# Reading the moving operand of every 512-column product in turn from the two halves of its columns

## The chip, the cores and the metric

The kernel runs on one core of one Trainium2 chip. The metric is the device time of one execution in microseconds (us), from runs of the whole program. A profiled execution gives a span (first to last instruction), and its own time stands beside that span below. TensorE is called PE, its weight loads PEld, VectorE DVE, ScalarE ACT, GpSimd POOL, and SP is the engine that issues most DMAs.

## The reference

One encoder layer with three parallel branches, on two sequences of 256 tokens each (512 token columns in all), width 1024, in float32:

```python
h = _rmsnorm(x, attn_norm_gain)
proj = h @ w_in                      # -> gdn qkv, decay, gates, mla latents, memory query, merge gates
# branch A: conv + SiLU on q, k, v; bidirectional chunked gated delta rule, 8 heads; gated norm
o_gdn = _rmsnorm(o_fwd + o_bwd, gdn_norm_gain) * silu(z_gdn)
# branch B: latent attention, 8 heads, rotary part; branch C: 4-head attention into 256 memory tokens
merged = (gates[:, :, 0] * (o_gdn @ w_br_gdn)
          + gates[:, :, 1] * (o_mla @ w_br_mla)
          + gates[:, :, 2] * (o_mem @ w_br_mem))
y = _rmsnorm(x + merged @ w_out, final_norm_gain)
```

## The kernel before

**Layout.** Activations are feature-major: a tile holds 128 features as partitions and all 512 tokens as columns. Each operand of a large product is split into a high and a low float32r part, and a product is the sum of three: high x high, low x high and high x low. `gemm` (L234) makes one 128x512 output tile: it loads a piece of weights (`weight`, L199: a DMA to `wr`, ACT rounds it to `wh`, DVE makes the remainder `wl`), then issues 3 x nk matmuls into one PSUM bank, nk being the number of 128-row blocks of the contraction (8, 4, 3 or 2). The weights are the stationary operand (128 columns, loaded anew for every matmul) and the activations `xs[k][j]` the moving operand, 512 columns read one after the other. There are 97 such tiles with nk = 8, 8 with nk = 4, 12 with nk = 3, 8 with nk = 2, and the narrow one of the rotary key: 2,604 matmuls at L246. The other 512-column products have the same form: `mem_v` (L399, 96), `mla_v` (L688, 48), the decay products of `gdn_prep` (L809, 8), `kk` in `gdn_in` (L971, 96) and the output projection (L1256, 168, and 48 more of 256 columns). `mem_v`, `mla_v` and the output projection have the weights as moving operand and the tokens as stationary one.

**Stages.** `front` (0 to 369 us in the profile) computes the memory keys and values, the norm, the latents and both attentions, with product tiles from a list `self.fill` put between the attention's steps. `middle` (369 to 761 us) runs the delta rule. `back` (from 761 us) multiplies the eight `xg` tiles (the normed delta-rule output of each head) by the branch weights (`bg`), merges and runs the output projection `y`. The tiles `bm` (branch B's projection) are the last of the fill list; `gemm` puts the matmuls of `bg` that need `xg7` last within each tile: 21 of 24 come before them.

**Order of PE in the middle.** It is written out by hand in `weave` (L1513). Chains of dependent steps are generators: `lane` 0 and 1 (the solves of the even and the odd heads), `heads_load`, `heads_in`, `heads_out`, `heads_norm`. A step yields two numbers, the PE time that it takes and the time until its next step is due, both in us of a clock that the planner keeps (`self.now`). While the next due step lies in the future, matmuls of the fill list are issued, each of which moves that clock on by the number that `gemm` yields:

```python
            if at[c] > self.now:
                cost = next(fill, None)
                self.idle += at[c] - self.now if cost is None else 0
                self.now = at[c] if cost is None else self.now + cost
```

When nothing of the list may be issued, the planner's clock jumps to the next due step. PE itself executes the order that results and waits only for true results. The due times on which the steps named later rest: head h is loaded once head h-3 has been read out (`while h > self.out + 2`), and counts as loaded 11 us later; `gdn_in` then has due times of 2.5, 2, 8, 6, 6 and 3 us; `gdn_solve` 7 and 7.5, then 6.5 us after each of seven steps (`u`, `xs`, `us`, `x`, `u`, `xs`, `us`); `gdn_out` (`o`, L1121) follows, 13 us after head 7's `o` comes its sum of squares `so` (L1137), and `gdn_norm` 10 and 6 us later. The fill list has conditions too (`can`, L1502): the `bm` tiles wait for all parts of `xa`; the last part is loaded once head 7's first `u` is due (`7 in self.started`) and may be split `XAT` = 14 us after that.

Of the kernel before, what the change touches and what calls it, by code (L numbers as in the profile page):

```python
# [31 lines left out]
        w.reshape(k // P, P, c // P, P).transpose(2, 1, 0, 3)).reshape(c // P, P, k)  # L32

def _pieces(w):

    k, c = w.shape
    return np.ascontiguousarray(
        w.reshape(k // 256, 2, P, c // 512, 512).transpose(3, 0, 2, 1, 4)).reshape(
            c // 512, k // 256, P, 1024)  # L40

def _consts():
# [42 lines left out]
def prep(i):  # L86

    f = {k: np.asarray(v) for k, v in i.items()}
    x = np.concatenate([f["x_prompt"][0], f["x_sample"][0]], 0)
    mem = np.concatenate([f["mem_prompt"][0], f["mem_sample"][0]], 0)  # L90
    w = f["w_in"][0]

    def fm(a):
        return np.ascontiguousarray(a.T.reshape(KD, P, T).transpose(1, 0, 2))

    def tm(a):
        return np.ascontiguousarray(a.reshape(4, P, D).transpose(1, 0, 2))

    def col(a):
        return np.ascontiguousarray(a.reshape(-1, P).T)  # L100

    qu = f["w_q_up"][0].reshape(384, 8, 192)
    rope = [qu[:, 4 * g:4 * g + 4, 128 + 32 * h:160 + 32 * h].reshape(384, P)
            for g in range(2) for h in range(2)]
    ku = f["w_kv_up"][0].reshape(256, 8, 256)
    mkv = f["w_mem_kv"][0]
    w8 = np.concatenate([
        _chunks(mkv[:, :512]),
        _chunks(w[:, O_QKV:O_QKV + 3072]),
        _chunks(w[:, O_ZG:O_ZG + 1024]),  # L110
        _chunks(w[:, O_CQ:O_CQ + 384]),
        _chunks(w[:, O_CKV:O_CKV + 256]),
        _chunks(w[:, O_ZM:O_ZM + 1024]),
        _chunks(w[:, O_QM:O_QM + 512]),
        _chunks(w[:, O_ZE:O_ZE + 512]),
        _chunks(w[:, O_G:O_G + 3072]),
        _chunks(f["w_br_gdn"][0]), _chunks(f["w_br_mla"][0])], 0)
    kr = np.concatenate([w[:, O_CKV + 256:O_CKV + 320], w[:, O_AB:O_AB + 32]], 1)
    kr = np.ascontiguousarray(kr.reshape(KD, P, 96).transpose(1, 0, 2)).reshape(P, KD * 96)
    prm = np.concatenate([  # L120
        col(f["attn_norm_gain"][0]), col(f["mem_norm_gain"][0]),
        f["conv_w"][0].reshape(5, 24, P).transpose(2, 1, 0).reshape(P, 120),
        np.broadcast_to(f["a_log"][0].reshape(1, 16), (P, 16)),
        np.broadcast_to(f["dt_bias"][0].reshape(1, 16), (P, 16)),
        col(f["gdn_norm_gain"][0]), col(f["q_norm_gain"][0]), col(f["kv_norm_gain"][0])], 1)
    a = {
        "xT": fm(x), "xn": tm(x), "memT": fm(mem),
        "cst": _CST, "sum": _SUM, "prm": np.ascontiguousarray(prm), "rope": _rope_tables(),
        "w8": w8, "w4": _chunks(f["w_br_mem"][0]),
        "w3": np.concatenate([  # L130
            _chunks(np.ascontiguousarray(qu[:, :, :128]).reshape(384, 1024))]
            + [_chunks(r) for r in rope], 0),
        "w2": _chunks(np.ascontiguousarray(ku[:, :, :128]).reshape(256, 1024)),
        "wkr": kr,
        "wvm": _pieces(mkv[:, 512:])[0],
        "wv": _pieces(np.ascontiguousarray(ku[:, :, 128:]).reshape(256, 1024))[:, 0],
        "wo": _pieces(f["w_out"][0]),
        "fg": f["final_norm_gain"].reshape(1, D),
    }
    return {k: np.ascontiguousarray(v) for k, v in a.items()}  # L140
# [16 lines left out]
class Layer:  # L157
# [76 lines left out]
    def gemm(self, src, nk, xs, name, m=P, ps=None):  # L234

        nc = self.nc
        hi, lo = self.weight(src, nk * m, name)
        ps = self.ps_gm("gm_" + name) if ps is None else ps
        n = 0
        order = [(p, k) for p in ((hi, 0), (hi, 1), (lo, 0)) for k in range(nk)]  # L240
        last = {"bm": 5, "bg": 7, "qm": 4}.get(name[:2])
        if last:

            order.sort(key=lambda o: o[1] >= last)
        for (a, j), k in order:
            nc.tensor.matmul(ps[:m], a[:, k * m:(k + 1) * m], xs[k][j],  # L246
                             start=n == 0, stop=n == 3 * nk - 1)
            n += 1
            yield 0.234
        return ps  # L250

    def add_square(self, acc, src, k, eng=0):
# [103 lines left out]
    def mem_v(self):  # L356
# [28 lines left out]
        for k, (raw, wr) in enumerate(raws):  # L385
            hl = self.pk.tile([P, 2, 512], F32R, tag="kq", bufs=8, name=f"mh{k}")
            hi = self.p0.tile([P, 1024], F32R, tag="wh", bufs=2, name=f"wh_vm{k}")
            lo = self.p0.tile([P, 1024], F32R, tag="wl", bufs=2, name=f"wl_vm{k}")
            if k:
                nc.scalar.activation(hi[:, :512], wr, AF.Copy)  # L390
            else:
                nc.vector.tensor_scalar(hi[:, :512], wr, 1.0, None, ALU.mult)
            rnd = self.split(raw, hl[:, 0], hl[:, 1], self.mg[:, k:k + 1])
            nc.vector.tensor_tensor(lo[:, :512], wr, hi[:, :512].bitcast(F32), op=ALU.subtract)
            ms.append((hl[:, 0], hl[:, 1]))
            for i, (a, b) in enumerate(((0, hi), (1, hi), (0, lo))):
                for tb in range(4):
                    t = slice(tb * P, (tb + 1) * P)
                    nc.tensor.matmul(vps[tb], ms[k][a][:, t], b[:, :512],  # L399
                                     start=k == 0 and i == 0, stop=k == 7 and i == 2)  # L400
            with self.tc.issue_after(rnd.ins) if k == 0 else nullcontext():
                self.add_square(acc, raw, k, 1)
# [21 lines left out]
    def mem_kt(self, h):  # L424
            nc, A, ms, rb = self.nc, self.A, self.mem_xs, self.rb
            ps = self.gemm_fm(A["w8"][C_KM + h], 8, ms, f"km{h}")
            kt = self.tb(f"kmt{h}")
            nc.scalar.activation(kt, ps, AF.Copy)
            nc.vector.tensor_tensor(kt, kt, rb, op=ALU.mult)
            t = self.big(h, f"km{h}")  # L430
            hi, lo = t[:, 0], t[:, 1]
# [57 lines left out]
    def rotate(self, dst, src, table):  # L489

        n = table.shape[0]
        self.nc.vector.tensor_tensor(dst.rearrange("p (s t) -> p s t", s=2), src.rearrange("p (s t) -> p s t", s=2),
                                     table.unsqueeze(1).to_broadcast([n, 2, 256]), op=ALU.mult)

    def rope_key(self):

# [9 lines left out]
        nc.scalar.activation(abT[64:96], ps[64:96], AF.Copy)  # L506
        t = self.tb("krt")
        u = self.tb("kru")
        self.rotate(t[0:64], ps[0:64], cs[0:64])
        self.rotate(u[0:32], ps[32:64], sn[32:64])  # L510
        self.rotate(u[32:64], ps[0:32], sn[0:32])
        nc.vector.tensor_tensor(t[0:32], t[0:32], u[0:32], op=ALU.subtract)
        nc.vector.tensor_tensor(t[32:64], t[32:64], u[32:64], op=ALU.add)
        self.ks1 = self.pa.tile([P, 512], F32R, name="ks1")
# [135 lines left out]
    def mla_rope(self, g):  # L650
# [5 lines left out]
        qs2 = self.pa.tile([P, 2, 512], F32R, tag="qs2", bufs=1, name=f"qs2{g}")  # L656
        for j, (p1, p2, op) in enumerate(((pa, pb, ALU.subtract), (pb, pa, ALU.add))):
            t, u = self.tb("rt"), self.tb("ru")
            self.rotate(t, p1, self.cos)
            self.rotate(u, p2, self.sin)  # L660
            nc.vector.tensor_tensor(t, t, u, op=op)
            hi = self.pa.tile([P, 512], F32R, tag="Qn", bufs=4, name=f"rh{g}{j}")
            lo = self.pa.tile([P, 512], F32R, tag="Qn", bufs=4, name=f"rl{g}{j}")
# [11 lines left out]
    def mla_v(self, g):  # L675
# [4 lines left out]
        for tb in range(4):  # L680
# [4 lines left out]
            n = 0  # L685
            for a, j in ((hi, 0), (hi, 1), (lo, 0)):
                for k in range(2):
                    nc.tensor.matmul(ps, self.kl[k][j][:, t], a[:, k * 512:(k + 1) * 512],  # L688
                                     start=n == 0, stop=n == 5)
                    n += 1  # L690
            vh = self.pa.tile([P, 512], F32R, tag="V", bufs=8, name=f"vh{g}{tb}")
# [4 lines left out]
    def mla_qk(self, hh, between):  # L696
        A = self.A
        r = []
        for w, nk, xs, n in ((A["w2"], 2, self.kl, "kn"), (A["w3"], 3, self.ql, "qn")):
# [6 lines left out]
            else:  # L706
                hi = self.pa.tile([P, 512], F32R, tag="Qn", bufs=4, name=f"{n}h{hh}")
                lo = self.pa.tile([P, 512], F32R, tag="Qn", bufs=4, name=f"{n}l{hh}")
            self.split(ps, hi, lo)
            r += [hi, lo]  # L710
        return r

# [64 lines left out]
    def gdn_prep(self, g):  # L777
# [12 lines left out]
        for d in range(2):  # L790
# [15 lines left out]
            yield 0.0, 4.0  # L806
            dp = self.ps_ms(d, f"dp{g}{d}")
            for i in range(2):
                nc.tensor.matmul(dp, self.bd, rhs[i], start=i == 0, stop=i == 1)  # L809
            nc.vector.tensor_tensor(ed, ed, dp, op=ALU.add)  # L810
            nc.scalar.activation(ed, ed, AF.Exp)
            eds.append(ed.rearrange("p (w i) -> p w i", i=32))
            yield 0.47, 0.0
# [125 lines left out]
    def gdn_in(self, hh):  # L939
# [24 lines left out]
        for s in range(2):  # L964
            pc = []
            hi, lo = hl[s]
            for cch in range(2):
                k = slice(cch * P, (cch + 1) * P)
                ps = self.ps_kk(f"kk{hh}{s}{cch}")
                for i, (a, b) in enumerate(((hi, hi), (hi, lo), (lo, hi))):  # L970
                    nc.tensor.matmul(ps, a[:, k], b, start=i == 0, stop=i == 2)  # L971
                pc.append(ps.rearrange("p (a t) -> p a t", a=2))
                yield 0.70, 6.0 * cch
            for a in range(2):
                for d in range(2):
                    for cp in range(2):
# [224 lines left out]
    def branch_mem(self, d):  # L1201
# [1 line left out]
        nc = self.nc  # L1203
        gt = yield from self.gate(2, d)
        ps = yield from self.gemm(self.A["w4"][d], 4, self.xe, f"be{d}")
        nc.vector.scalar_tensor_tensor(gt, gt, 1.0, ps, ALU.add, ALU.mult)
        nc.sync.dma_start(self.d_m[d], gt)

    def gate_in(self, j, d):
# [12 lines left out]
    def gated(self, d, gt, ps):  # L1222

        nc = self.nc
        nc.vector.scalar_tensor_tensor(gt, gt, 1.0, ps, ALU.add, ALU.mult)  # L1225
        nc.gpsimd.tensor_tensor(self.merged[d], self.merged[d], gt, op=ALU.add)  # L1226

    def branch(self, j, d, xs, w, name):
# [4 lines left out]
    def output(self):  # L1233
# [17 lines left out]
        def product(ps, hi, lo, j, tb, c0=0, c1=512):  # L1251
            t = slice(tb * P, (tb + 1) * P)
            n = 0
            for q in range(2):
                for a, b in ((0, hi), (1, hi), (0, lo)):
                    nc.tensor.matmul(ps, xs[2 * j + q][a][:, t], b[:, q * 512 + c0:q * 512 + c1],  # L1256
                                     start=j == 0 and n == 0, stop=j == 3 and n == 5)
                    n += 1

# [355 lines left out]
```

## Time and profile before

| what | value |
|---|---|
| median of 3 runs | 859.25 us (858.84 to 859.51) |
| profiled execution | 859.05 us, its span 857.3 us |
| PE busy | 845.6 us (99%), 4,822 matmul records |
| PEld / DVE / ACT / POOL busy | 698.4 / 573.4 / 451.9 / 145.4 us |
| mean DMA rate | 135 GB/s |
| granted TensorE clock | 0.999 |

A matmul's recorded duration is longer than the distance to the next one, since matmuls overlap in the pipeline; the price of one is read from the starts of successive rows. One product of plain float32 operands shows as two matmul records. In rows of the timeline neighbouring instructions of one kind are merged: `x8` are eight of them, and the first number is the first one's start. A name such as `gm_qkv` is the output of the tile `qkv`.

### The profile page before, as it was taken

The numbers are of one execution on the slowest core, as the hardware profiler recorded it, in microseconds if no ns is written. First come the engines' busy times: TensorE is split into PE (matmuls) and PEld (weight loads), VectorE is DVE, ScalarE is ACT, GpSimd is POOL, SyncE is SP. The second block draws the span as 40 slices with busy tenths as digits, with TensorE's granted clock in tenths as the row PEclk, the third lists the DMA queues.
The fourth block names the chain that finished last, engine by engine and source line by source line (L and its number), as shares of the span: only waits on it lengthen the run. The fifth ranks groups of instructions, "written<-read, shape, count | busy, mean of one in ns | idle before, by whom it ended". The sixth has DMA issues, their size and how long they took to land.

```text
span 857.3 us, 13230 instructions
## 1 busy us (share of the span) xinstructions
PE 845.6 (99%) x4822; PEld 698.4 (81%) x4822; DVE 573.4 (67%) x1021; ACT 451.9 (53%) x891; POOL 145.4 (17%) x135
## 2 busy tenths in 40 slices
PE   9999999999999999999999999999999999999997
PEld 7878888888888888878788888888888888888886
DVE  7776347687599998457689998684555544346543
ACT  7655455455474465546775748666663632223232
POOL 0200111000100002072101254213110002332121
PEclk9999999999999999999999999999999999999999
DMA  9422222442425525363334365546445447375332
GB/s 326 141 79 87 86 81 68 139 138 75 103 77 164 137 90 146 116 191 129 109 103 122 117 189 174 152 134 180 132 122 160 138 134 250 118 241 160 116 98 99
DMA packets 68273, 116.10 MB, mean 135 GB/s; under 512 B 24048, under 2 KB 31600, under 8 KB 68208
## 3 DMA queue, kind: packets, MB, share of 16 engines
q1 hardware_dynamic: 46560, 104.51, 38.6%
q10 hardware_dynamic: 21648, 10.75, 4.6%
q8 instruction: 38, 0.62, 0.3%
q14 instruction: 27, 0.22, 0.1%
HBM read 95.09 MB, written 16.99 MB: 131 GB/s over the span
## 4 chain that ended last, share of the span: by engine, by line
PE 95%; DVE 2%; ACT 1%; issue 1%; DMA 1%; POOL 0%; POOLq 0%; ACTq 0%; DVEq 0%; SPq 0%
PE gm_qkv L246 16%; PE gm_g L246 16%; PE gm_z L246 8%; PE gm_bm L246 5%; PE gm_bg L246 5%; PE gm_za L246 5%; PE y L1256 5%; PE vm L399 3%; PE gm_be L246 3%; PE gm_qm L246 3%; PE gm_km L246 3%; PE kk L971 3%; PE o L1121 2%; PE gm_qn L246 2%; PE gm_cq L246 2%; PE s_a L308 2%
## 5 line engine op out<-in xcount | busy, mean ns | idle before, releaser
L745 DVE SCALAR_TENSOR_TENSOR kq<-cz,prm,kq 128x510 f32<-128x510 f32 (+1 forms) x64 | 48.1, 752 | 6.0 <-ACT kq L738 5.0
L246 PE MATMUL gm_qkv<-hh,wh_qkv 128*128 128x512 f32 x192 | 51.1, 400 | 0.5 <-ACT wh_qkv L210 0.5
L246 PE MATMUL gm_g<-hl,wh_g 128*128 128x512 f32 x192 | 51.5, 399 | 0.0
L246 PE MATMUL gm_g<-hh,wl_g 128*128 128x512 f32 x192 | 51.3, 398 | 0.0
L246 PE MATMUL gm_g<-hh,wh_g 128*128 128x512 f32 x192 | 51.1, 401 | 0.1
L246 PE MATMUL gm_qkv<-hh,wl_qkv 128*128 128x512 f32 x192 | 50.3, 397 | 0.0
L246 PE MATMUL gm_qkv<-hl,wh_qkv 128*128 128x512 f32 x192 | 49.7, 396 | 0.0
L214 DVE TENSOR_TENSOR wl_qkv<-wr_qkv,wh_qkv 128x1024 fp32r<-128x1024 f32 x24 | 31.1, 1297 | 25.9 <-ACT wh_qkv L210 10.1
L214 DVE TENSOR_TENSOR wl_g<-wr_g,wh_g 128x1024 fp32r<-128x1024 f32 x24 | 30.1, 1254 | 22.0 <-PE gm_g L246 11.7
L246 PEld LDWEIGHTS gm_qkv<-hl,wh_qkv 128*128 128x128 f32 x192 | 35.8, 188 | 8.2
L246 PEld LDWEIGHTS gm_qkv<-hh,wh_qkv 128*128 128x128 f32 x192 | 35.3, 188 | 8.9 <-ACT wh_qkv L210 1.2
L246 PEld LDWEIGHTS gm_qkv<-hh,wl_qkv 128*128 128x128 f32 x192 | 35.5, 188 | 7.8
L246 PEld LDWEIGHTS gm_g<-hl,wh_g 128*128 128x128 f32 x192 | 35.4, 188 | 7.7
L246 PEld LDWEIGHTS gm_g<-hh,wl_g 128*128 128x128 f32 x192 | 35.3, 188 | 7.5
L246 PEld LDWEIGHTS gm_g<-hh,wh_g 128*128 128x128 f32 x192 | 35.1, 188 | 7.8 <-ACT wh_g L210 0.3
L210 ACT ACTIVATE wh_qkv<-wr_qkv 128x1024 fp32r<-128x1024 f32 x24 | 25.4, 1058 | 29.1 <-PE gm_qkv L246 8.6
L1256 PE MATMUL y<-wh_wo,mh 128*128 128x512 f32 (+1 forms) x144 | 39.9, 370 | 0.0
L210 ACT ACTIVATE wh_g<-wr_g 128x1024 fp32r<-128x1024 f32 x24 | 25.4, 1060 | 26.0 <-PE gm_g L246 11.6
L961 POOL TENSOR_TENSOR kl<-kq,kh 128x512 fp32r<-128x512 f32 x16 | 22.8, 1427 | 94.8 <-ACT kh L959 94.8
L1226 POOL TENSOR_TENSOR mg<-mg,lg 128x512 f32<-128x512 f32 x16 | 27.2, 1700 | 59.0 <-DVE lg L1225 59.0
L246 PE MATMUL gm_bm<-xa,wh_bm 128*128 128x512 f32 x128 | 33.5, 398 | 0.0
L246 PE MATMUL gm_bg<-xg,wh_bg 128*128 128x512 f32 x128 | 32.5, 395 | 0.0
(432 smaller groups left out, 2199.5 us busy)
## 6 DMA issues: line engine op xcount, KB each, us to landing
wr_g<-in_w_dram SPq DMA_DIRECT2D x24, 512.0 KB
wr_qkv<-in_w_dram SPq DMA_DIRECT2D x24, 512.0 KB
e<-d_r SPq DMA_DIRECT2D x64, 96.0 KB
wr_z<-in_w_dram SPq DMA_DIRECT2D x12, 512.0 KB
d_g<-gt_g ACTq DMA_DIRECT2D x16, 256.0 KB
wr_za<-in_w_dram SPq DMA_DIRECT2D x8, 512.0 KB
wr_bm<-in_w_dram SPq DMA_DIRECT2D x8, 512.0 KB
lg<-d_g SPq DMA_DIRECT2D x16, 256.0 KB
```

Source lines behind the costliest of these rows:

```text
L210: self.wround = nc.scalar.activation(hi[:, :n], raw[:, :n], AF.Copy).ins
L214: d = eng.tensor_tensor(lo[:, :n], raw[:, :n], hi[:, :n].bitcast(F32), op=ALU.subtract)
L246: nc.tensor.matmul(ps[:m], a[:, k * m:(k + 1) * m], xs[k][j], start=n == 0, stop=n == 3 * nk - 1)
L308: nc.tensor.matmul(sp[:, qb * 256:(qb + 1) * 256], a, b, start=j == 0, stop=j == n - 1)
L399: nc.tensor.matmul(vps[tb], ms[k][a][:, t], b[:, :512], start=k == 0 and i == 0, stop=k == 7 and i == 2)
L745: nc.vector.scalar_tensor_tensor(ys, zs, self.cw[:, f, m:m + 1], ys, ALU.mult, ALU.add)
L961: nc.gpsimd.tensor_tensor(lo, src, hi.bitcast(F32), op=ALU.subtract)
L971: nc.tensor.matmul(ps, a[:, k], b, start=i == 0, stop=i == 2)
L1121: nc.tensor.matmul(out, ub[:, d, s, cp], rhs, start=n == 0, stop=n == 3)
L1226: nc.gpsimd.tensor_tensor(self.merged[d], self.merged[d], gt, op=ALU.add)
L1256: nc.tensor.matmul(ps, xs[2 * j + q][a][:, t], b[:, q * 512 + c0:q * 512 + c1], start=j == 0 and n == 0, stop=j == 3 and n == 5)
```

## The change

The moving operand of each 512-column product is given as a three-dimensional pattern: column 0 of the first half, column 0 of the second half, column 1 of the first, and so on (`turns`). The output is written to PSUM in the order in which columns arrive, one column after the other (`pairs` gives the output the same shape). So output column 2s + c holds moving column 256c + s. Where the columns were put apart beforehand (even columns in the first half, odd ones in the second), the output has its natural order: the host does that for `xT` and for the weight pieces that are moving operands. Elsewhere the readers of the PSUM tile take it with a step of two elements (`unpaired`) and write natural order (`halves`). Numbers of instructions, DMAs, tiles and buffers are the same. The planner's cost of one matmul goes from 0.234 to 0.217 and that of three `kk` products from 0.70 to 0.65. The attention's 256-column products and the plain-float32 products of the delta rule are not touched.

```diff
+def _halves(a):
+    return np.concatenate([a[..., 0::2], a[..., 1::2]], -1)
 def _pieces(w):
-        w.reshape(k // 256, 2, P, c // 512, 512).transpose(3, 0, 2, 1, 4)).reshape(
+        _halves(w.reshape(k // 256, 2, P, c // 512, 512)).transpose(3, 0, 2, 1, 4)).reshape(
+def turns(x):
+    return x.rearrange("p (c s) -> p s c", c=2)
+def pairs(x):
+    return x.rearrange("p (s c) -> p s c", c=2)
+def halves(x):
+    return x.rearrange("p (c s) -> p c s", c=2)
+def unpaired(x):
+    return x.rearrange("p (s c) -> p c s", c=2)
...
-        "xT": fm(x), "xn": tm(x), "memT": fm(mem),
+        "xT": _halves(fm(x)), "xn": tm(x), "memT": fm(mem),
...
-            nc.tensor.matmul(ps[:m], a[:, k * m:(k + 1) * m], xs[k][j],
+            nc.tensor.matmul(pairs(ps[:m]), a[:, k * m:(k + 1) * m], turns(xs[k][j]),
-            yield 0.234
+            yield 0.217
...
-                    nc.tensor.matmul(vps[tb], ms[k][a][:, t], b[:, :512],
+                    nc.tensor.matmul(pairs(vps[tb]), ms[k][a][:, t], turns(b[:, :512]),
...
-            nc.scalar.activation(kt, ps, AF.Copy)
+            nc.scalar.activation(halves(kt), unpaired(ps), AF.Copy)
...
-            self.rotate(t, p1, self.cos)
-            self.rotate(u, p2, self.sin)
+            self.rotate(t, unpaired(p1), self.cos)
+            self.rotate(u, unpaired(p2), self.sin)
...
-                    nc.tensor.matmul(ps, self.kl[k][j][:, t], a[:, k * 512:(k + 1) * 512],
+                    nc.tensor.matmul(pairs(ps), self.kl[k][j][:, t], turns(a[:, k * 512:(k + 1) * 512]),
...
-            self.split(ps, hi, lo)
+            self.split(unpaired(ps), halves(hi), halves(lo))
...
-                nc.tensor.matmul(dp, self.bd, rhs[i], start=i == 0, stop=i == 1)
-            nc.vector.tensor_tensor(ed, ed, dp, op=ALU.add)
+                nc.tensor.matmul(pairs(dp), self.bd, turns(rhs[i]), start=i == 0, stop=i == 1)
+            nc.vector.tensor_tensor(halves(ed), halves(ed), unpaired(dp), op=ALU.add)
...
-                    nc.tensor.matmul(ps, a[:, k], b, start=i == 0, stop=i == 2)
-                pc.append(ps.rearrange("p (a t) -> p a t", a=2))
-                yield 0.70, 6.0 * cch
+                    nc.tensor.matmul(pairs(ps), a[:, k], turns(b), start=i == 0, stop=i == 2)
+                pc.append(unpaired(ps))
+                yield 0.65, 6.0 * cch
...
-        nc.vector.scalar_tensor_tensor(gt, gt, 1.0, ps, ALU.add, ALU.mult)
+        nc.vector.scalar_tensor_tensor(halves(gt), halves(gt), 1.0, unpaired(ps), ALU.add, ALU.mult)
...
-                    nc.tensor.matmul(ps, xs[2 * j + q][a][:, t], b[:, q * 512 + c0:q * 512 + c1],
+                    nc.tensor.matmul(pairs(ps), xs[2 * j + q][a][:, t],
+                                     turns(b[:, q * 512:(q + 1) * 512])[:, c0 // 2:c1 // 2],
```

More of the change, by code (lines that the diff above doesn't have):

```diff
@@ L491, in rotate @@
         n = table.shape[0]
-        self.nc.vector.tensor_tensor(dst.rearrange("p (s t) -> p s t", s=2), src.rearrange("p (s t) -> p s t", s=2),
-                                     table.unsqueeze(1).to_broadcast([n, 2, 256]), op=ALU.mult)
+        self.nc.vector.tensor_tensor(halves(dst), src, table.unsqueeze(1).to_broadcast([n, 2, 256]), op=ALU.mult)
     def rope_key(self):
@@ L508, in rope_key @@
         u = self.tb("kru")
-        self.rotate(t[0:64], ps[0:64], cs[0:64])
-        self.rotate(u[0:32], ps[32:64], sn[32:64])
-        self.rotate(u[32:64], ps[0:32], sn[0:32])
+        self.rotate(t[0:64], halves(ps[0:64]), cs[0:64])
+        self.rotate(u[0:32], halves(ps[32:64]), sn[32:64])
+        self.rotate(u[32:64], halves(ps[0:32]), sn[0:32])
         nc.vector.tensor_tensor(t[0:32], t[0:32], u[0:32], op=ALU.subtract)
@@ L1224, in gated @@
         nc = self.nc
-        nc.vector.scalar_tensor_tensor(gt, gt, 1.0, ps, ALU.add, ALU.mult)
+        nc.vector.scalar_tensor_tensor(halves(gt), halves(gt), 1.0, unpaired(ps), ALU.add, ALU.mult)
         nc.gpsimd.tensor_tensor(self.merged[d], self.merged[d], gt, op=ALU.add)
```

## The prediction

> **What bounds the kernel now.** I read the page first, then the timeline of PE for the price of one product, then the chain of work for the order of the middle, then stages by window.
>
> ```profile
> span 857.3 us, 13230 instructions
> PE 845.6 (99%) x4822; PEld 698.4 (81%) x4822; DVE 573.4 (67%) x1021; ACT 451.9 (53%) x891; POOL 145.4 (17%) x135
> PE 95%; DVE 2%; ACT 1%; issue 1%; DMA 1%; POOL 0%; POOLq 0%; ACTq 0%; DVEq 0%; SPq 0%
> ```
>
> PE is busy 99% of the span and holds 95% of the chain that ended last. So the price of a product is the price of the kernel, unless something else takes over. That price, from the timeline:
>
> ```profile
> 300.76 0.40 PE L308 MATMUL s_a<-ks,qs 128*128 128x256 f32 x2
> 301.00 0.40 PE L308 MATMUL s_a<-kn,qnh 128*128 128x256 f32 x2
> ...
> 302.78 2.03 PE L246 MATMUL gm_za<-hh,wh_za 128*128 128x512 f32 x8
> 304.65 2.03 PE L246 MATMUL gm_za<-hl,wh_za 128*128 128x512 f32 x8
> 306.51 2.03 PE L246 MATMUL gm_za<-hh,wl_za 128*128 128x512 f32 x8
> 308.38 0.86 PE L246 MATMUL gm_qn<-qlh,wh_qn 128*128 128x512 f32 x3
> ```
>
> From 302.78 to 308.38 are 24 products: 233.3 ns each. A 256-column one takes 0.24 / 2 = 120 ns. So the price is (233.3 - 120) / 256 = 0.443 ns per column and some 7 ns fixed.
>
> Is that the most that PE can do? The plain-float32 products of the read-out tell:
>
> ```profile
> L1121 PE MATMUL o<-e,ub 128*128 128x256 f32 x64 | 19.3, 383 | 0.0
> L1121 PE MATMUL o<-e,ub 128*128 128x128 f32 x64 | 12.3, 274 | 0.0
> 475.16 2.83 PE o L1121 x16
> 507.18 2.62 PE o L1121 x16
> ...
> 588.03 2.81 PE o L1121 x16
> 620.03 2.62 PE o L1121 x16
> ...
> 701.08 2.62 PE o L1121 x16
> 732.93 2.62 PE o L1121 x16
> ```
>
> The 8 heads issue 32 products of 256 and 32 of 128 columns and the trace has 64 of each: two records per product. One head's 16 records bring 8 x 256 + 8 x 128 = 3,072 columns in 2.62 us, 0.853 ns a column. I read a record as two passes over its columns, since the ratio to 0.443 is near two: 0.426 ns a column, 218 ns for 512 with fixed costs included. So PE streams faster when each operand element is used in more than one pass, and the float32r products lose some 16 ns per 512 columns on what feeds them. The loss is there where DVE and ACT are half idle as well:
>
> ```profile
> 820.92 0.39 PE L1256 MATMUL y<-wl_wo,mh 128*128 128x512 f32 x1
> ...
> 822.55 2.49 PE L1256 MATMUL y<-wh_wo,mh 128*128 128x512 f32 x10
> ...
> 806.00:846.00 40.00, 40.00 (x177) 32.50 (x177) 17.72 (x24) 13.46 (x23) 7.94 (x7) 1.00 0.29 97
> ```
>
> 820.92 to 822.55 are 7 products, 233 ns each, with DVE at 17.72 and ACT at 13.46 of 40 us (fourth and fifth numbers) and the full clock (1.00). So it is no contention with other engines; it belongs to the reading of the moving operand, which is what the change touches.
>
> **The change, part by part.**
>
> *The rate.* No row has a moving operand read in turn, so I bound it. Lower end: 217 ns, the rate of the read-out. Upper end: the slowest 512-column stream here,
>
> ```profile
> 1.49 4.28 PE L367 MATMUL zp<-zero 128*128 128x512 f32 x10 [1.49 <-DVE zero L364]
> ```
>
> about 428 ns, at start-up. I take 217: the loss is proportional to columns and goes with the order of feeding, and the read-out shows the array itself able to do it. Saving 16.3 ns on each of 3,020 products (counts in the source: 2,604 + 96 + 48 + 8 + 96 + 168), 49.2 us, and by the 120-ns row about 8 ns on 48 of 256 columns, 0.4 us. [...]
>
> But the saving does not arrive everywhere; by stage:
>
> ```profile
> 0.00:369.40 369.40, 280.82 (x1117) 205.01 (x1118) 1.00 0.39 121
> 369.40:686.00 316.60, 255.00 (x1022) 187.66 (x1022) 1.00 0.47 144
> 369.40:710.40 341.00, 275.34 (x1104) 202.70 (x1104) 1.00 0.46 142
> ```
>
> (windows of L246 alone; the count is behind PE's busy time).
>
> *Front.* 1,117 + 96 + 48 + 4 = 1,265 products x 16.3 = 20.6 us. DVE is nearly full in places:
>
> ```profile
> 240.00:280.00 40.00, 38.80 (x206) 32.65 (x205) 38.79 (x81) 23.63 (x49) 0.00 (x0) 1.00 0.43 126
> 280.00:320.00 40.00, 40.00 (x195) 33.07 (x194) 36.35 (x78) 22.23 (x43) 0.91 (x1) 1.00 0.39 109
> 440.00:480.00 40.00, 40.00 (x288) 32.91 (x287) 37.44 (x80) 25.95 (x62) 5.22 (x4) 1.00 0.40 124
> 480.00:520.00 40.00, 40.00 (x231) 33.45 (x230) 37.77 (x78) 22.86 (x48) 19.18 (x19) 1.00 0.50 151
> ```
>
> From 240 to 320 us DVE needs 75.1 us; at the new rate PE would pass that stretch in about 75. I take off 3 us for waits on DVE, here and where attention steps have less cover. Front: 17.6 us.
>
> *Middle.* Here the planner's due times rule, and they stay. The `o` rows of heads three apart: 475.16 to 588.03, 507.18 to 620.03, 588.03 to 701.08, 620.03 to 732.93, always 112.9 us: load, 11, gdn_in's and gdn_solve's due times, read-out, load again. A faster fill product does not shorten that: more of them go into the same gaps, and the list runs dry sooner. So from the middle's start to head 7's `o` nothing is gained. Before the first `bm` 1,104 products go; at 0.217 they and the shorter `kk` steps fill the gaps that 1,021 fill now, up to about 686. Then:
>
> ```profile
> 681.66 0.61 PE L1078 MATMUL u<-vs,y 128*128 128x128 f32 x4
> 748.47 0.95 PE L1137 MATMUL so<-cst,sq 128*128 128x1 f32 x8
> 759.97 0.69 DVE L226 SCALAR_TENSOR_TENSOR xg<-og,xg 128x512 fp32r<-128x512 f32 x1 [0.70 <-ACT xg L222]
> 761.03 3.43 PE L246 MATMUL gm_bg<-xg,wh_bg 128*128 128x512 f32 x14
> 765.93 0.63 PE L246 MATMUL gm_bg<-xg,wh_bg 128*128 128x512 f32 x2
> ```
>
> `bm` waits for head 7's first `u` (681.7) and 14 us: 695.7 by the plan. In that hole PE has only solve steps; it waits for their true results, which come sooner than the due 6.5 us. I count 6 of the 9.7 us: `bm` from 692. Its 192 products take 41.7 us, the steps among them about 10 (two `o` of 2.62, the rest from 0.4 to 0.9): 743.7. That uses up the cover behind head 7: `so`, planned 13 us behind `o`, now comes after all `bm`. From its end (749.4) to `xg7` (760.7) now pass 11.3 us under cover; then 755. `bg`'s first 21 products last 4.6 us, so PE waits about 6.7 us and the first product on `xg7` starts at 755 instead of 766: 11 us; 7.3 if the whole hole counts. I take 9, less 1.5 for DVE, whose 75.2 us between 440 and 520 meet denser fill: 7.5 us.
>
> *Back.* 171 products of `bg` and 168 of `y`, 339 x 16.3 = 5.5, and 0.4: 5.9 us.
>
> *Readers of PSUM with a step of two.* 24 tiles' ACT and DVE reads, 24 gate products, `dp`, and 128 `kk` reads; not shown, bounded by
>
> ```profile
> L982 DVE SCALAR_TENSOR_TENSOR na<-e,cc,kk 128x256 f32<-128x256 f32 x32 | 15.2, 475 | 8.2 <-PE kk L971 8.1
> L858 DVE TENSOR_TENSOR nd<-nd,kd 128x512 f32<-128x512 f32 x2 | 1.4, 680 | 0.0
> L856 DVE TENSOR_TENSOR dd<-nd,kd 128x512 f32<-128x512 f32 x2 | 2.2, 1099 | 0.0
> ```
>
> From 0 (the same elements, as L858) to 0.42 us per 512 (L856, which writes with a step of 32): DVE work of up to 40 us, spread; where DVE is full, up to 5 us of the time. A gain has no reason. Eight bytes are nearer to none than to 128: I take 0. *Host layout* is outside the measured time; DMAs, queues and weight loads stay (188-ns loads overlap).
>
> *Sum.* 17.6 + 7.5 + 5.9 = 31.0 us: span 826.3; the profiled execution has 1.75 us around its span (859.05), and the median is 0.2 above it: 828 us.
>
> **The rivals.**
>
> *All of it arrives* (49.6 us, 809.5): the true steps of the middle would have to run well ahead of the plan, or the tail after `o` be covered. For it: PE waits only for results. Against: the plan's order puts fill between steps.
>
> *Half the loss goes* (225 ns): front 8.8, back 3; in the middle PE sets the pace until `so`: 1,396 x 8.3 = 11.6 less, then the uncovered 12.2 and not 5: 5 gained. 842. For it: nothing shows that all of the loss is one cause.
>
> *The turn changes nothing at 233 ns.* Then the plan is wrong for it: `so` still comes after all `bm`, at 761, and `xg7` at 773; the first product on it starts 7.2 us late: 866.
>
> *Slower products.* If the loss is paid for each fetch of neighbouring columns, the turn needs more fetches: twice as many cost another 16.3 ns, 249.6 ns and +49 +7: 915. It decides from 7.2 / 3,020 = 2.4 ns below today's price, 231 ns. For it: the extra is per column already; against: no row. [...]
>
> **How the numbers follow.** Forecast 60% (span of its own, 820 to 837: hole and waits at either bound); all arrives 10%; half 13%; no change in rate 6%; slower products 11%. Forecast, all and half are 83%: 809 to 845. A change within 0.2% (1.7 us, what a measurement here tells from none) needs a mixture, 2% from the edge of the last two; slower 15%, faster 83%.
>
> **What would show it.** Eight products in 1.74 us instead of 1.87 (rate); `o` rows still 112.9 us apart (middle); a PE gap of some 5 us before `bg`'s products on `xg7`, ended by DVE at L226, and gaps around 690; L982 still near 475 ns (readers). Wrong if a 512-column product stays above 225 ns, or if `o` rows come closer together.

## The result, and the profile after

The changed kernel takes 829.25 us (median of four runs, 826.32 to 831.36) against 859.38 us (858.84 to 860.04) for the kernel before. The ratio is 0.9647, with a 95% interval from 0.9616 to 0.9677: faster by 30.1 us. The profiled execution took 829.28 us, its span 827.5. The forecast was 828. The total is right to 1.3 us; the way to it inside the middle stage was not.

Line numbers of the changed kernel are higher by 24 or 25: L246 is now L271, L982 is L1006, L1121 is L1145, L1256 is L1280; L1121 in rows of the changed kernel is the solve step `us`. First the page of the changed kernel: span, busy times, and shares of the chain that ended last.

```profile
span 827.5 us, 13240 instructions
PE 799.8 (97%) x4822; PEld 701.0 (85%) x4822; DVE 569.5 (69%) x1021; ACT 448.1 (54%) x891; POOL 141.3 (17%) x135
PE 76%; DVE 8%; ACT 5%; DMA 5%; issue 3%; POOL 1%; SPq 1%; ACTq 0%; POOLq 0%; DVEq 0%
```

PE is busy for 45.8 us less, but the span fell by 29.8 only. PE's share of the chain went from 95% to 76%; DVE's went from 2% to 8%, and ACT's and the DMAs' from 1% to 5% each. So about 46 us were offered, and 16 of them, a third, went into waits that were not there before.

The price of a product, from PE's timeline of the changed kernel (start, length of the group, the instructions):

```profile
305.77 1.89 PE L271 MATMUL gm_za<-hh,wh_za 128*128 128x512 f32 x8
307.50 0.59 PE L271 MATMUL gm_za<-hl,wh_za 128*128 128x512 f32 x2
```

From 305.77 to 307.50 are 8 products in 1.73 us: 216 ns each, where it was 233. That much is as forecast (1.74 for 8). On 3,020 products 17.3 ns are 52 us; of the 6 us that PE's busy time does not show, 1.7 are found below (half the clock), and the rest is not placed. Where the products' saving ended up, by stage, in us (the boundaries are the end of the last `oa`, the first `bg` product and the first `y` product on PE's timeline):

| stage | before | after | gained | forecast |
|---|---|---|---|---|
| front, to the last `oa` | 369.4 | 352.7 | 16.7 | 17.6 |
| middle, to the first `bg` | 391.6 | 380.8 | 10.8 | 7.5 for these two, |
| `bg` | 44.8 | 45.9 | -1.1 | and 2.8 for `bg`'s rate |
| `y` to the end of the span | 51.5 | 48.2 | 3.3 | 3.1 |

Where PE waits, from the list of waits (the waiting instruction, what it waits for, us in total, times, the longest). The kernel before has its two longest in the front and none in the middle:

```profile
PE zp L367 <- DVE zero L364: 1.5, 1, 1.5
PE oa L343 <- DVE za L727: 1.1, 1, 1.1
```

The changed kernel:

```profile
PE us L1121 <- DVE w L1116: 2.5, 2, 1.5
PE kd L847 <- DVE kq L771: 2.5, 1, 2.5
PE gm_bg L271 <- ACT xg L247: 2.3, 1, 2.3
PE kk L995 <- DVE zt_z L1187: 2.3, 1, 2.3
PE gm_g L271 <- ACT wh_g L235: 1.8, 1, 1.8
PE gm_qkv L271 <- ACT wh_qkv L235: 1.6, 2, 1.3
```

The first four are waits of the middle and of `bg`, and three of them are on DVE. A first window of the changed kernel is 400 to 480 us; a second, of the kernel before, lies as far behind its last `oa` (us, then busy time of PE, PEld, DVE, ACT, POOL, then PE's granted clock):

```profile
400.00:480.00 80.00, 77.18 (x663) 67.22 (x663) 76.63 (x161) 50.64 (x113) 13.66 (x11) 1.00 0.36 110
417.00:497.00 80.00, 80.00 (x646) 65.74 (x633) 75.77 (x159) 51.47 (x114) 15.36 (x13) 1.00 0.37 118
```

DVE is busy for 76.6 of these 80 us, but it was so for 75.8 before, and PE never stood idle. So here a full DVE alone did not make PE wait; what counted is when single results came. Shortly before the wait for `kd` (402.7 to 405.2 us), and as the one for `zt_z` (562.5 to 564.8 us) began, DVE itself stood idle, as its rows show:

```profile
398.16 0.75 DVE L769 SCALAR_TENSOR_TENSOR kq<-cz,prm,kq 128x510 f32<-128x510 f32 x1 [4.71 <-ACT kq L762]
...
563.24 0.69 DVE L1177 TENSOR_TENSOR og<-og,rob 128x512 f32<-128x512 f32 x1 [1.73 <-DMA rob<-d_n]
563.97 0.69 DVE L1187 SCALAR_TENSOR_TENSOR zt_z<-zt_z,gm_z 128x512 f32<-128x512 f32 x1
```

In the first case DVE had waited 4.7 us for ACT to start the convolution of `kq`. In the second, `zt_z` stood behind an instruction that waited 1.7 us for a DMA.

The tail of the middle, from PE's timeline of the changed kernel:

```profile
682.21 0.68 PE L1121 MATMUL us<-w,y 128*128 128x128 f32 x4 [1.52 <-DVE w L1116]
...
733.43 3.18 PE L271 MATMUL gm_bg<-xg,wh_bg 128*128 128x512 f32 x14
736.45 1.67 PE L271 MATMUL gm_bg<-xg,wl_bg 128*128 128x512 f32 x7
737.96 3.19 PE L271 MATMUL gm_bg<-xg,wh_bg 128*128 128x512 f32 x14
740.98 1.67 PE L271 MATMUL gm_bg<-xg,wl_bg 128*128 128x512 f32 x7
744.98 1.61 PE L271 MATMUL gm_bg<-xg,wh_bg 128*128 128x512 f32 x3 [2.32 <-ACT xg L247]
746.38 0.63 PE L271 MATMUL gm_bg<-xg,wl_bg 128*128 128x512 f32 x1
```

The hole before `bm` has one wait of 1.5 us in it, not 6. The first 21 products of two `bg` tiles, 42 in all, go before the first product on `xg7`, not 21; so the wait there is 2.3 us, not 6.7. But what follows that wait is slow: 3 products in 1.40 us, from 744.98 to 746.38. The window of the changed kernel behind the wait, with the granted clock third from the end:

```profile
745.05:748.46 3.41, 3.41 (x8) 2.24 (x9) 1.79 (x3) 1.79 (x2) 0.59 (x1) 0.50 0.46 190
```

After the wait PE ran for 3.41 us at half the clock, which costs another 1.7 us.

The readers of PSUM that now step by two take no longer. The group of the 256-column reads of the changed kernel (busy us, mean ns):

```profile
L1006 DVE SCALAR_TENSOR_TENSOR na<-e,cc,kk 128x256 f32<-128x256 f32 x32 | 15.2, 474 | 6.8 <-PE kk L995 6.8
```

It was 475 ns with neighbouring elements. ACT's reads of the same kind (`qnh`, L247) take 586 ns on the mean, 591 before.

### The profile page after: what moved, and what is told of

Its sections match the earlier page's. It is cut to its first block, busy times and chain, and to the rows that moved or that the text cites. A ratio compares the mean times of both kernels' runs of the same rounds, so it can differ in the third digit from the quotient of the medians.

```text
span 827.5 us, 13240 instructions
## 1 busy us (share of the span) xinstructions
PE 799.8 (97%) x4822; PEld 701.0 (85%) x4822; DVE 569.5 (69%) x1021; ACT 448.1 (54%) x891; POOL 141.3 (17%) x135
## 4 chain that ended last, share of the span: by engine, by line
PE 76%; DVE 8%; ACT 5%; DMA 5%; issue 3%; POOL 1%; SPq 1%; ACTq 0%; POOLq 0%; DVEq 0%
PE gm_g L271 13%; PE gm_qkv L271 12%; PE gm_z L271 5%; PE y L1280 4%; PE gm_za L271 4%; PE gm_bg L271 4%; PE gm_bm L271 3%; PE gm_be L271 3%; PE gm_qm L271 3%; PE gm_km L271 3%; PE kk L995 2%; PE s_a L333 2%; PE vm L424 2%; PE o L1145 2%; PE gm_cq L271 2%
## 5 line engine op out<-in xcount | busy, mean ns | idle before, releaser
L271 PE MATMUL gm_g<-hh,wh_g 128*128 128x512 f32 x192 | 47.7, 385 | 2.3 <-ACT wh_g L235 1.8
L271 PE MATMUL gm_qkv<-hh,wh_qkv 128*128 128x512 f32 x192 | 47.1, 382 | 1.6 <-ACT wh_qkv L235 1.6
L271 PE MATMUL gm_g<-hl,wh_g 128*128 128x512 f32 x192 | 47.9, 384 | 0.0
L271 PE MATMUL gm_g<-hh,wl_g 128*128 128x512 f32 x192 | 47.8, 382 | 0.0
L271 PE MATMUL gm_qkv<-hl,wh_qkv 128*128 128x512 f32 x192 | 47.4, 382 | 0.0
L271 PE MATMUL gm_qkv<-hh,wl_qkv 128*128 128x512 f32 x192 | 47.0, 380 | 0.0
L239 DVE TENSOR_TENSOR wl_qkv<-wr_qkv,wh_qkv 128x1024 fp32r<-128x1024 f32 x24 | 30.2, 1258 | 19.5 <-PE gm_za L271 5.1
L271 PEld LDWEIGHTS gm_g<-hh,wh_g 128*128 128x128 f32 x192 | 35.5, 189 | 7.9 <-ACT wh_g L235 2.4
L271 PEld LDWEIGHTS gm_qkv<-hh,wh_qkv 128*128 128x128 f32 x192 | 35.7, 189 | 7.2 <-ACT wh_qkv L235 2.4
L271 PEld LDWEIGHTS gm_qkv<-hh,wl_qkv 128*128 128x128 f32 x192 | 35.9, 189 | 5.0
L271 PEld LDWEIGHTS gm_g<-hl,wh_g 128*128 128x128 f32 x192 | 35.8, 189 | 4.8
L271 PEld LDWEIGHTS gm_qkv<-hl,wh_qkv 128*128 128x128 f32 x192 | 35.7, 189 | 4.7
L271 PEld LDWEIGHTS gm_g<-hh,wl_g 128*128 128x128 f32 x192 | 35.5, 189 | 4.6
L1280 PE MATMUL y<-wh_wo,mh 128*128 128x512 f32 (+1 forms) x144 | 37.7, 356 | 0.0
L769 DVE SCALAR_TENSOR_TENSOR vf<-cz,prm,vf 128x510 f32<-128x510 f32 (+1 forms) x32 | 26.3, 822 | 12.1 <-ACT vf L762 11.9
L271 PE MATMUL gm_bg<-xg,wh_bg 128*128 128x512 f32 x128 | 31.7, 392 | 2.3 <-ACT xg L247 2.3
```

Source lines behind the costliest of these rows:

```text
L239: d = eng.tensor_tensor(lo[:, :n], raw[:, :n], hi[:, :n].bitcast(F32), op=ALU.subtract)
L271: nc.tensor.matmul(pairs(ps[:m]), a[:, k * m:(k + 1) * m], turns(xs[k][j]), start=n == 0, stop=n == 3 * nk - 1)
L769: nc.vector.scalar_tensor_tensor(ys, zs, self.cw[:, f, m:m + 1], ys, ALU.mult, ALU.add)
L1280: nc.tensor.matmul(pairs(ps), xs[2 * j + q][a][:, t], turns(b[:, q * 512:(q + 1) * 512])[:, c0 // 2:c1 // 2], start=j == 0 and n == 0, sto ...
```

## The experiments

Two questions were open: what in the feeding of the moving operand makes a product 216 ns long, and what took a third of the saving away. For the second there were two theories that do not exclude each other: the order of the plan (its prices of 0.217 and 0.65 in the place of 0.234 and 0.70), and results of DVE that come late between 400 and 565 us.

### The moving operand by itself

`m1_forms` runs 16 groups of 24 products of 512 columns, twice, and nothing else on PE:

```python
def turn(c):    # c streams in turn; "turn2" is what the change does
    return lambda x: x.rearrange("p (c s) -> p s c", c=c)
def step(c):    # one stream with a step of c
    return lambda x: x.rearrange("p (s c) -> p c s", c=c)
def near(s):    # two streams in turn, s columns apart
    return lambda x: x.rearrange("p (b c s) -> p b s c", c=2, s=s)
def group(d):   # d columns of one half, then d of the other; "duo", "quad"
    return lambda x: x.rearrange("p (c s d) -> p s c d", c=2, d=d)
```

> This kernel computes nothing of the layer: it runs 24 float32r products of 512 columns for each of 16 ways of reading the moving operand, twice over (the second time in reverse order), with the weights loaded anew for each product as in the layer. Named by their output tile: plain (one column after the other), turn2, turn4, turn8 (in turn from 2, 4, 8 equal parts of the row: 1024, 512, 256 bytes apart), near4 to near128 (in turn from two neighbouring blocks of 4 to 128 columns: 16 to 512 bytes apart), step2, step4, step8 (a step of 2, 4 or 8 columns, so 8, 16, 32 bytes), duo and quad (2 or 4 neighbouring columns from either half in turn), few (plain, with 32 weight columns in place of 128). Expected, plain: 232 to 234 ns, turn2: 216. Theory A, the loss of 16 ns comes from two successive reads that lie close together in the row: every way whose successive reads are far apart has 216 (turn4, turn8, near64, near128, step8), those with reads within 16 bytes have 233 (near4, step2), quad stays near 233, and duo lies between. [...]

From PE's timeline of this kernel, second pass. The `turn_1z` of 11.86 us has eight streams. The three rows of `step_1z` are steps of 8, 4 and 2. The row of `near_1z` holds the six distances from 128 down to 4 columns. The last two `turn_1z` are four streams and two.

```profile
129.50 11.86 PE L86 MATMUL turn_1z<-h,wh 128*128 128x512 f32 x24
141.18 5.73 PE L86 MATMUL few_1z<-h,wh 128*32 128x512 f32 x24
146.75 6.17 PE L86 MATMUL quad_1z<-h,wh 128*128 128x512 f32 x24
152.75 8.04 PE L86 MATMUL duo_1z<-h,wh 128*128 128x512 f32 x24
160.61 10.52 PE L86 MATMUL step_1z<-h,wh 128*128 128x512 f32 x24
170.95 11.26 PE L86 MATMUL step_1z<-h,wh 128*128 128x512 f32 x24
182.02 11.02 PE L86 MATMUL step_1z<-h,wh 128*128 128x512 f32 x24
192.85 31.26 PE L86 MATMUL near_1z<-h,wh 128*128 128x512 f32 x144
224.23 6.68 PE L86 MATMUL turn_1z<-h,wh 128*128 128x512 f32 x23
230.97 5.13 PE L86 MATMUL turn_1z<-h,wh 128*128 128x512 f32 x23
235.93 5.64 PE L86 MATMUL plain_1z<-h,wh 128*128 128x512 f32 x24
```

From start to start, per product: eight streams 487 ns, quad 250, duo 328, steps of 8, 4 and 2 431, 461 and 451, `near` 216 on the mean of the six distances (192.85 to 224.23 less one product of four streams, 31.10 / 144), and each of them 216 when its 24 are counted alone, four streams 283, two 216 (4.96 / 23). Plain is 227 in the median, and 232 with 32 weight columns.

Theory A falls, and plain was expected at 232 to 234. It is not the distance between the two places, since 16 bytes apart is as quick as 1,024 (216 ns both), and four streams, 512 bytes apart, take 283. It is not a charge for each jump in the row alone: steps of 4 and 8 columns are slower than plain, at 461 and 431, but `turn2` jumps at each column and is among the quickest. Fewer weight columns do not do it either: a straight read with a quarter of them takes 232 and not 216. What stands is a fact without a mechanism: two streams read in turn, column by column, take 216 ns, and every other form tried takes more. All quick forms have an innermost dimension of two columns, as `duo` has too; a straight read written in that shape was not run, so the shape of the pattern is not told apart from the order of the reads.

Plain products take 227 ns here and 233 in the layer. So some 6 of the 17 ns gained come with what surrounds the products there; with what exactly is not settled. Two streams take 216 in both.

### The change with the old prices of the plan

```diff
-            yield 0.217
+            yield 0.234
-                yield 0.65, 6.0 * cch
+                yield 0.70, 6.0 * cch
```

> The changed kernel with the planner's costs of before (0.234 and 0.70): PE's order in the middle is that of before, the reads are in turn. Theory A (due times of the plan used up the gain of the middle): the list no longer runs dry before bm, the cover behind head 7's o is back, all steps come 7 per cent sooner in true time: 819 to 824 us. Theory B (true results of DVE, ACT and DMAs come too late at the new rate, whatever the plan): as many waits as now or more, 828 to 834 us. If nothing but the rate mattered: 809.5 us.

Measured: 818.98 us (818.25 to 819.5), ratio 0.9531, 0.9518 to 0.9544. It is 10.3 us faster than the change itself and the fastest whole kernel here. This kernel's window from 400 to 500:

```profile
400.00:500.00 100.00, 98.70 (x782) 86.19 (x781) 96.52 (x198) 62.48 (x136) 31.50 (x27) 1.00 0.44 132
```

DVE is at 96.5 of 100 us and PE at 98.7; the change has 96.2 for PE in the same window. So DVE is fuller here than in the change (89.3), and PE waits less: the busy share does not tell whether results are late. `kd` and `xg7` are not waited for at all, and there is no stretch at half the clock but the last one of the span (mean granted clock 0.998; 0.996 in the change). The `o` of head 7 starts 348.0 us after the last `oa`, where it is 363.3 before and 363.0 after the change.

### The new prices without the change

The kernel before, with 0.217 and 0.65 in its plan and nothing else:

```diff
-            yield 0.234
+            yield 0.217
-                yield 0.70, 6.0 * cch
+                yield 0.65, 6.0 * cch
```

> The kernel of before with the planner's new costs (0.217 and 0.65) and nothing else: products stay at 233 ns. The prediction's price for this was 866 us (+7.2, the sum of squares of head 7 comes after all bm, and its xg7 is waited for). After the changed kernel's trace, where two tiles of bg and not one stand before the first product on xg7, less: 861 to 865 us. Rival, the plan and not the rate made the kernel faster: under 855 us.

Measured: 863.94 us (863.72 to 866.18), ratio 1.0061, 1.0047 to 1.0075. Slower by 4.6 us, 3.9 of it in the middle and 0.8 in `bg`. Head 7's `o` starts 376.6 us after the last `oa`, 13.3 later than with the old prices. This is the forecast's rival "the turn changes nothing", which it put at 866. The number is near, but not by its reason, a wait for `xg7`: there is none here. The waits of the middle are 1.7 us for `kd` and 1.5 before `bm`.

Together the four combinations say how prices act. Due times of the plan (11, 6.5 and so on) are in the plan's microseconds, and between two steps it puts as many products as fill them at its price. A lower price puts more products between two steps. The forecast had it that with equal rates and prices the steps of a head stay apart by the same true time. The rows don't show that head by head (see the middle, below). With a price above the true rate the whole chain of heads is drawn together.

### The norm of head 7 earlier

```diff
-        yield 0.0, 13 if hh == 7 else 11
+        yield 0.0, 6 if hh == 7 else 11
```

> The changed kernel with head 7's sum of squares due 6 us after its read-out in place of 13. If the wait of 2.3 us for xg7 and the 3.4 us at half clock behind it cost time, both go: 825 us (4 less). If so or xg7 is late for another reason, or the time is lost elsewhere: 829 us.

Measured: 826.66 us (824.13 to 828.55), ratio 0.9617, 0.9601 to 0.9633: 2.6 us less than the change, but the two intervals overlap, and 826.7 lies between the two times expected. What the edit does is read from the profiled execution. `bg` takes 41.4 us in the place of 45.9, so the wait and the half clock are gone, 4.4 us in all. But the middle took 2.4 longer: the wait for `kd` is still there, and here it is followed by half the clock. A window of this kernel, right behind the wait for `kd`:

```profile
405.31:408.72 3.41, 3.41 (x39) 2.81 (x36) 2.08 (x6) 1.06 (x1) 1.18 (x1) 0.50 0.41 147
```

So the place that the forecast named for the new wait was right, and mending it is worth 4.4 us there in this execution; the half clock accounts for 1.7 of the 2.4 lost elsewhere.

### Less work for DVE

Two of the four added taps of the convolution are left out for heads 4 to 7, so that the outputs are not the reference's. That is 24 DVE instructions (997 in the page, 1021 in the change) and 15.3 us of DVE's busy time (554.2 against 569.5), once with the change's prices and once with the old ones:

```diff
-        for m in (1, 3, 0, 4):
+        for m in (1, 3, 0, 4)[:2 if f % 8 >= 4 else 4]:
```

> The changed kernel with two of the four added taps of the convolution left out for heads 4 to 7 (the tiles of the middle; its outputs are not the reference's): 24 DVE instructions of about 0.75 us fewer, 18 us of DVE work, most of it between 400 and 570 us, where DVE is full. Theory A (the plan's due times set the middle): the waits of PE there go, some 8 us, but PE reaches the steps of heads 6 and 7 that much sooner and waits for their results, so the middle shrinks by 2 to 4 us: 825 to 827. Theory B (DVE's lateness is what the gain was lost to): the waits go and the time with them: 819 to 822.

Measured: 820.0 us (819.08 to 821.07), ratio 0.9544, 0.9531 to 0.9557: 9.3 us less than the change. This kernel's window from 400 to 500:

```profile
400.00:500.00 100.00, 100.00 (x785) 87.94 (x785) 89.02 (x182) 63.47 (x136) 30.01 (x26) 1.00 0.48 142
```

PE is never idle from 400 to 500 us. In the list of waits the one for `kd` and that of `kk` on `zt_z` are gone, and the one for `xg7` is down from 2.3 to 0.5 us. Head 7's `o` starts 355.3 us after the last `oa`, 7.7 sooner, and the middle lasts 373.0 in the place of 380.8; `bg` takes 43.3 in the place of 45.9. So these taps are worth about 9 us to the change, as the plan is worth about 10; the two are not to be added, as the next run shows. Leaving taps out does two things at once: DVE has less to do, and the chain from a product to `kq` and `vf` is shorter. Which of the two it is, this pair of runs does not tell.

> The same two taps left out in the changed kernel with the planner's costs of before (819.0 us). Its middle takes 374.5 us, about 7 more than products at 216 ns account for. If that rest is DVE's: 812 to 814 us. If it is true results of the solve steps and of the loads: 817 to 819.

Measured: 813.74 us (812.48 to 816.06), ratio 0.9473, 0.9459 to 0.9488. With the old prices the same relief of DVE is worth 5.2 us, and with DVE relieved the old prices are worth 6.3. Both together are worth 15.5 us, where the sum of each alone is 19.5, so they overlap by 4 us. That this is where a step that the plan puts late also finds DVE late is likely, but not shown.

### Prices further up and down

0.250 and 0.75, then 0.210 and 0.63, in the two lines of the first experiment on the plan.

> The changed kernel with the planner's costs of a product at 0.250 and of three kk products at 0.75. Fewer products stand in each gap of the plan, so that the steps come sooner in true time (a due time of 6.5 us is 5.6 us of products at 216 ns). Theory A: as long as the results are there by then, more cover is left for the end, and the time is that of 0.234 (819) or a little less, 816 to 820. Theory B: true results come too late already at 0.217, so tighter steps wait more: 825 or more.

Measured: 825.01 us (820.67 to 826.9), ratio 0.9594, 0.9574 to 0.9615: 6.0 us slower than with 0.234, in runs that differ by 6 us among themselves. Head 7's `o` comes still sooner, 334.9 us after the last `oa`, but PE now waits for DVE inside the middle. From this kernel's list of waits, and its window from 400 to 500:

```profile
PE kk L995 <- DVE e L1006: 4.4, 2, 4.0
...
400.00:500.00 100.00, 94.60 (x755) 81.98 (x754) 93.97 (x197) 60.63 (x136) 29.69 (x25) 0.98 0.42 120
```

PE is idle for 5.4 us in this window, 1.3 with 0.234. Two stretches of 3.41 us at half the clock, behind 489 and 353 us, cost this execution some 3.4 us more.

> The changed kernel with the planner's costs at 0.210 and 0.63: more products in each gap than PE really does in that time. Theory A: the list runs dry still sooner, less cover at the end, 832 to 838 us. Theory B: steps come later in true time and wait less: 824 to 829.

Measured: 837.18 us (836.64 to 839.9), ratio 0.9757, 0.9742 to 0.9773. Head 7's `o` starts 368.5 us after the last `oa`. This is where the forecast's two holes really open. From this kernel's list of waits, the wait for `xg7` and the one before `bm`, then a window at half the clock at each of the two, `bm` first; they begin 1.9 and 4.0 us before the waits end, at 682.29 and 752.62 us:

```profile
PE gm_bg L271 <- ACT xg L247: 7.0, 1, 7.0
PE us L1121 <- DVE w L1116: 4.3, 1, 4.3
...
680.39:687.22 6.83, 4.93 (x18) 4.48 (x19) 2.05 (x4) 2.14 (x5) 0.00 (x0) 0.50 1.05 406
...
748.65:755.48 6.83, 2.86 (x7) 1.81 (x7) 2.10 (x4) 1.76 (x3) 0.00 (x0) 0.50 0.16 38
```

Four prices give 837, 829, 819 and 825 us. The best of the four lies above the true price of 0.216. With lower prices the waits grow behind head 7 (2.3 and 7.0 us for `xg7`, none with 0.234); with 0.250 they grow inside the middle, on DVE (4.0 us in one).

### Work moved from DVE to POOL

With the old prices, eight of the `wl` subtractions of the middle go to POOL:

```diff
-            eng = nc.vector
+            eng = nc.gpsimd if name in ('z28', 'z29', 'z30', 'z31', 'g10', 'g11', 'g12', 'g13') else nc.vector
```

> The kernel with reads in turn and the planner's costs of before (819.0 us), with the subtraction that makes wl moved from DVE to POOL for eight tiles of the middle (z28 to z31 and g10 to g13): about 9.8 us of DVE work less where DVE is full (400 to 500 us), and POOL, idle three quarters of that time, gets eight instructions of 2.5 to 3 us. If the rest of the middle's loss is DVE's amount of work, 815 to 817 us. If POOL's other work there (kl, the copies of the solve tables) or DVE's waiting on POOL's reads eats it, 819 or more.

Measured: 828.67 us (827.52 to 830.15), ratio 0.9646, 0.9632 to 0.9659: 9.7 us slower than without it. That is the second of the two outcomes expected (819 or more), which named no upper end. The groups of this kernel:

```profile
L239 POOL TENSOR_TENSOR wl_g<-wr_g,wh_g 128x1024 fp32r<-128x1024 f32 x4 | 10.3, 2585 | 10.6 <-ACT wh_g L235 7.2 <-ACT ub L1124 3.5
L769 DVE SCALAR_TENSOR_TENSOR kq<-cz,prm,kq 128x510 f32<-128x510 f32 (+1 forms) x64 | 53.3, 832 | 7.2 <-ACT kq L762 6.4
L895 DVE TENSOR_TENSOR tm<-xx,tt 128x31 f32<-128x31 f32 (+15 forms) x62 | 28.3, 456 | 1.0
```

and the same two DVE groups of the kernel with the old prices alone:

```profile
L769 DVE SCALAR_TENSOR_TENSOR kq<-cz,prm,kq 128x510 f32<-128x510 f32 (+1 forms) x64 | 48.9, 765 | 5.1 <-ACT kq L762 4.4
L895 DVE TENSOR_TENSOR tm<-xx,tt 128x31 f32<-128x31 f32 (+15 forms) x62 | 23.1, 373 | 0.8
```

Eight instructions of about 1.2 us left DVE, 9.8 us. These two groups alone took 4.4 and 5.2 us back, and it is nine instructions that did it: five of `kq` and four of `tm` ran while a moved subtraction ran, by their starts and ends, and took 1.82 and 1.85 us on the mean; the others took 0.75 and 0.36. So DVE gained nothing (573.2 us busy, 570.0 without the move), and each of the eight results came later, after some 2.5 us on POOL. Whether DVE's amount of work is what the middle still loses, this run therefore can't tell.

## Why the prediction was right, and where it was not

*The rate.* Taken at 217 ns from the read-out's records; measured at 216 in every stage (8 products in 1.73 us from 121.90 in the front, 8 in 1.72 from 427.90 in the middle, 14 in 3.02 from 733.43 in `bg`, 5 in 1.07 from 784.47 in `y`). The bound was right. Its reasoning was in part luck: I read the read-out as a sign that more passes for one fetch run faster, and the forms show that nothing so simple holds, since four streams take 283 ns and not less than two (216). "No contention with other engines" holds only in part: straight reads with nothing else on PE take 227 ns, so some 6 of the 17 ns go with the layer around them.

*Front.* 17.6 forecast, 16.7 measured. At 17.3 ns saved the 1,265 products offer 21.9, so 5 us were lost and not 3; PE's idle time in the front rose from 5.3 to 9.2 us. What is named of it is mostly on weights that ACT rounds: `gm_g` waits 1.8 us for `wh_g`, `gm_qkv` 1.6 us for `wh_qkv` (0.5 before). I had allowed for waits on DVE and for less cover of attention steps; the rest of the 5 us is not placed.

*Middle.* Together with `bg`, 9.7 gained against 7.5 + 2.8 = 10.3. This is the step where the sum held and the terms did not. That the sum held is luck: the term for DVE was some 6 us too small, and the two holes were some 7 us too large.

- "From the middle's start to head 7's `o` nothing is gained": 363.3 us before, 363.0 after. That is true in the number, but not for the reason given. The `o` rows of heads three apart were to stay 112.9 us apart, and that sign failed. From the chain of the changed kernel:

```profile
495.30 2.62 PE o L1145 x16
532.00 2.62 PE o L1145 x16
582.51 1.31 PE o L1145 x8
...
612.84 2.62 PE o L1145 x16
650.00 1.31 PE o L1145 x8
...
682.89 2.62 PE o L1145 x16
```

  495.3 to 612.8 is 117.5 us and 532.0 to 650.0 is 118.0; then 582.5 to 682.9 is 100.4. Two errors cancel here. Up to head 5 the heads fall behind: its `o` comes 12.3 us later than before the change, counted from the last `oa`, and only 4.5 later with the two taps left out. Then they catch up, between the `o` of heads 5 and 6: 46.6 us before, 32.9 in the change, 32.9 also with fewer taps, 34.6 with the new prices alone, and 43.9 in the change with the old prices. So the catching up belongs to the new plan. It lies where no product of the list may be issued: from 679.6 to 685.3 us PE has only the steps `xs`, `us`, `us` and `o`. The planner's clock jumps there from one due time to the next, while PE waits only for results. The forecast said so of its hole, but did not count it for head 7's `o`.
- The term for DVE was 1.5 us. With the two taps left out the middle of the changed kernel is 7.7 us shorter, so this is the most mis-sized term of the sum. That shorter products leave DVE no time is not the whole of it, since DVE was as full before (75.8 of 80 us) without a wait; two of the late results come behind waits of DVE itself. Amount of work and length of the chain are not told apart.
- The hole before `bm` was to cost 6 us; its one longer wait is 1.5. The wait for `xg7` was to cost 6.7; it is 2.3 and 1.7 for the half clock behind it. In the count of its cover I took the 21 products that stand ahead in the kernel before; in the order built for the changed kernel two tiles' worth, 42, go first. Both holes are real, as the run with 0.210 shows them at 4.3 and 7.0 us; at 0.217 they are a quarter and some 60% of what I made them. I named DVE at L226 (now L251) as the releaser; the row names ACT at L247, which writes the first half of the pair that PE takes first.

*Back.* 5.9 forecast for `bg`'s rate, `y` and the rest; 3.1 of it for `y`, and 3.3 measured.

*Readers of PSUM.* Taken at 0 between 0 and 0.42 us; 474 ns against 475 in the largest group. Right.

*The rivals.* "All arrives" (809.5) did not come, and needed both a plan whose steps run ahead and a DVE that follows; old prices and fewer taps together reach 813.7, with a part of the work left out. "Half the loss goes" is excluded by the rate. "No change in rate" is the run with new prices alone, 863.9 against 866; the number was near, but the wait for `xg7` that was to make it did not come. "Slower products" did not come for two streams, but its concern was sound: four and eight streams (283 and 487 ns), steps (431 to 461), and pairs and fours of columns (328 and 250) are all slower than plain (227), the worst of them by a factor of two.

## What to carry to other kernels

When the price of the commonest instruction falls, look in every stage for the results that came just in time before, and price their chains against the shorter stage. An engine's busy share is only a first hint: here DVE was busy for 75.8 of 80 us before, without a wait, and for 76.6 after, with one of 2.5. A list scheduler's prices are knobs and not measurements: here a price 8% above the true one was worth 10 us, as due times are counted in it, so prices are to be swept again after such a change and not only corrected. An access pattern for the moving operand is to be measured in its exact form, since neighbours of the best form (four streams at 283 ns, pairs or fours of columns at 328 and 250) were slower here than no pattern at all (227).

## What the runs showed of the hardware that was not expected

- Float32r products of 512 columns take 216 ns when two streams, 16 to 1,024 bytes apart, are read in turn, and 227 to 233 when read straight.
- Half the clock after short waits. In two cases a wait of some 2.4 us was followed by 3.41 us at a granted clock of 0.50 (2.3 us before 745 us in the change, 2.5 before 405 us in the run with the norm of head 7 earlier), and one of 2.8 us before 448 us, in the run with POOL, by products some 0.42 us apart in the place of 0.22. A wait of 4.0 us was followed by 3.41 us at 0.50 too (price 0.250), and 6.83 us at 0.50 began within each of the waits of 4.3 and 7.0 us (price 0.210). Other waits of the same length were followed by none: behind those for `kd` and `kk` in the change (2.5 and 2.3 us) the granted clock is 1.00.
- Reads of PSUM with a step of 8 bytes by DVE took 474 ns, against 475 with neighbouring elements.
